# Decay mask of the state-space groups moved into a transfer, and exponentials moved from VectorE to ScalarE

## The chip, the cores and the metric

The kernel runs on one core of a Trainium2 chip. The metric is the time of one execution on the device in microseconds (us). The core's engines work through queues of their own: TensorE (PE, with its weight loads as PEld), VectorE (DVE), ScalarE (ACT), GpSimd (POOL) and SyncE (SP). Transfers are issued by SP, POOL and ACT and carried by 16 DMA engines.

## What is computed

One decoder layer over 512 tokens and 16 learned meta tokens ahead of them, 1024 wide: a normalised input is projected, goes through a pooling branch and a state-space branch (Mamba-2, "SSD"), and the gated sum of both is followed by a feed-forward block. The change lies in the state-space branch. It has 32 heads in 8 groups of 4, works in chunks of 128 tokens, and for each chunk computes

```
a_cs   = cumsum(a_dt)                                  # per head, within the chunk
lmat   = exp(where(l >= s, a_cs[l] - a_cs[s], -inf))   # decay from token s to token l
cb     = c_mat[l] . b_mat[s]                           # per group
y_diag = sum over s of cb * lmat * xdt[s]
y_off  = exp(a_cs[l]) * (c_mat[l] . state)             # state carried from chunk to chunk
y      = (y_diag + y_off + xs * d_skip) * silu(z)
y      = y * rsqrt(mean(y^2 over the group) + 1e-5)    # per group
```

## The kernel before, in words

The projections dominate. Their weights come in blocks of 128x1024 (`raw`, loaded by SP). ACT rounds each block to the upper part `whi` (L111), DVE subtracts to get the lower part `wlo` (L113), and PE multiplies both with the two parts of the input (L215, L218). The results go through a convolution (`conv`: ACT L437, three DVE steps L440, ACT Silu L442).

The eight groups run as `ssd(g)` (L591 to L724), woven with the projections of the next group, `group_proj(g+1)`: while ACT, DVE and POOL prepare group g, PE multiplies for group g+1. Sums of weights (POOL transfers L774 to L783 into `f_t` and `f_s`, among them accumulating ones, L781 and L783) and small copies `seen` that pace them (L797) share POOL's queue. The order of each engine's queue is fixed when the program is built; every engine then works through its own queue strictly in order, so an instruction that waits holds up all behind it.

In `ssd(g)` the path to the diagonal product is this:

- **abc** (128 x 4 x 512, f32; one buffer, so that group g's load has to wait for the last product `py` of group g-1) gets a_cs of the group's four heads, broadcast to all 128 partitions by one POOL transfer (L599). Free axis: token l. Partition: token s of the chunk.
- `eb` = exp(abc), two ACT instructions of 64 partitions each (L633), used by y_off.
- The differences a_cs[l] - a_cs[s], clamped at zero so that no exponential overflows: 8 pieces of 128x128 on ACT (Relu with negative scale, L638), 8 on DVE (L641). Then two exponentials of 128x1024 on ACT (L644, L645). `decay` holds these; in the last group (g7) it is placed behind the copy of the first state (`st`, L667).
- `cbm` = c.b (PE L656) times the triangular mask `tri` (DVE L658): this is where tokens l < s are cut off. Then abc is multiplied with cbm (DVE L676, 128x2048; in g7 in two halves).
- PE multiplies abc with `xdt` into `py` (L691), and the states with `ct` into `po` (L685).

The group's norm: squares and their sums (PE), a Sqrt on ACT (L712) and four reciprocals on DVE (L714) give the factor `rs`; then `yh`/`yl` (L721) are ready for the output product (`pso`, `psp`: L146 to L149).

ACT's functions lie in tables; a change of table shows in the trace as an instruction of its own, ACT_TABLE_LOAD, under the line of the function that needs it.

Of the kernel before, what the change touches and what calls it, by code (L numbers as in the profile page):

```python
# [11 lines left out]
AF = mybir.ActivationFunctionType  # L12
ALU = mybir.AluOpType

P = 128
# [6 lines left out]
G = 8  # L22
R = 4
# [26 lines left out]
X_PAIRS = (4, 5, 6, 7)  # L50
# [14 lines left out]
def kernel(ctx: ExitStack, tc, xT, x, w, fx, f1, f2, vec, fnw, out):  # L65
    nc = tc.nc
    act, dve, pe, pool = nc.scalar, nc.vector, nc.tensor, nc.gpsimd
# [33 lines left out]
    def after(*ins):  # L101
        st = ExitStack()
        for i in ins:
            if i is not None:
                st.enter_context(tc.issue_after(i.ins))
        return st
# [36 lines left out]
    def mm3s(ps, pairs, first=True, last=True):  # L143
# [4 lines left out]
        for n, ((ah, al), (bh, bl)) in enumerate(pairs):  # L148
# [9 lines left out]
    tri = const.tile([P, P], F32, name="tri")  # L158
    pool.affine_select(out=tri, in_=ones_f, compare_op=ALU.is_ge, fill=0.0, base=0,
                       pattern=[[1, P]], channel_multiplier=-1)  # L160
    eps = const.tile([P, 1], F32, name="eps")
    dve.memset(eps, EPS)
    vs = const.tile([P, V_N], F32, name="vs")
# [5 lines left out]
    dtok = const.tile([P, 2, 4, HEADS], F32, name="dtok")  # L169
# [26 lines left out]
    def psum1(name):  # L196
        return psb.tile([P, 512], F32, tag="s", name=name)
# [139 lines left out]
    pn = psum1("pn1")  # L337
    for c in range(6):
        pe.matmul(pn[:NT, c : c + 1], q[:, c * NT : (c + 1) * NT], ones_f[:, :1], start=True, stop=True)
    rs = pre.tile([NT, 6], F32, name="rs")  # L340
# [12 lines left out]
    for i in range(2):  # L353
        pb = psum1(f"pb1_{i}")
        c = slice(3 * i, 3 * i + 3)
# [14 lines left out]
    for c in range(4):  # L370
        r = slice(c * H, (c + 1) * H)
# [22 lines left out]
    acs_d = dram.tile([H, SEQ], F32, name="acs_d")  # L394
    for c in range(4):
        nc.gpsimd.dma_start(acs_d[:, c * P : (c + 1) * P], acs[c * H : (c + 1) * H, :P])
    def dt_out():

        sel = pre.tile([P, 2, P], F32, tag="wdt", name="sel")
        dve.tensor_copy(sel[:, 0, :], ident[:, P - 1 : P].to_broadcast([P, P]))  # L400
        dve.tensor_copy(sel[:, 1, :], ident[:, NM - 1 : NM].to_broadcast([P, P]))
        pt = psum1("pt_dt")
        for j, src in enumerate((dt, acs)):
            pe.transpose(pt[:, j * P : (j + 1) * P], src[:, :P], ident)
            pe.transpose(pt[:NM, 256 + j * H : 256 + (j + 1) * H], src[:H, P:], ident[:H, :H])
        dve.tensor_copy(dtok.rearrange("p a c h -> p (a c h)"), pt[:, :256])
        dve.tensor_copy(dtm.rearrange("p a h -> p (a h)"), pt[:NM, 256 : 256 + 2 * H])
        pq = psum1("pq_dt")
        pe.matmul(pq[:, :128], sel[:, 0, :], dtok[:, 1, :, :].rearrange("p c h -> p (c h)"),
                  start=True, stop=True)  # L410
        pe.matmul(pq[:NM, 128 : 128 + H], sel[:NM, 1, :NM], dtm[:, 1, :], start=True, stop=True)
        fl = lambda t: t.rearrange("p c h -> p (c h)")
        dve.tensor_tensor(fl(dec), pq[:, :128], fl(dtok[:, 1, :, :]), op=ALU.subtract)
        dve.tensor_tensor(wmeta[:NM], pq[:NM, 128 : 128 + H], dtm[:, 1, :], op=ALU.subtract)
        act.activation(fl(dec), fl(dec), AF.Exp)
        act.activation(wmeta[:NM], wmeta[:NM], AF.Exp)
        dve.tensor_tensor(wmeta[:NM], wmeta[:NM], dtm[:, 0, :], op=ALU.mult)
        act.activation(fl(cdec), pq[:, :128], AF.Exp)


    u_d = [dram.tile([P, L], F32, name=f"u_d{k}") for k in range(NK)]
# [10 lines left out]
    x_ready, z_ready, filled = {}, {}, {}  # L432
# [158 lines left out]
    def ssd(g, cur):  # L591

        xc, bt, ct, zt = cur
        hs = slice(R * g, R * g + R)
        tok = lambda c: slice(NM + c * P, NM + (c + 1) * P)
        ctok = lambda c: slice(c * P, (c + 1) * P)
        flat = lambda t: t.rearrange("p r d -> p (r d)")
        abc = gs.tile([P, R, SEQ], F32, tag="abc", name=f"abc{g}")
        abc_load[g] = nc.gpsimd.dma_start(abc, acs_d[hs, :].partition_broadcast(P))  # L599

        xdt = gs.tile([P, 4, R, 64], F32, tag="xdt", name=f"xdt{g}")
        btok = gs.tile([P, 4, P], F32, tag="btok", name=f"btok{g}")
# [23 lines left out]
        if g == G - 1:  # L626
            yield
        eb = gs.tile([P, 2, SEQ], F32, tag="eb", name=f"eb{g}")
        ap = abc.rearrange("p (i j) l -> p i j l", j=2)
        for j in range(2):  # L630
            js = slice(64 * j, 64 * j + 64)
            with after((z_ready if g in X_PAIRS else x_ready)[g], late_cast[0] if g == G - 1 else None):
                act.activation(eb[js, :, :], ap[js, :, j, :], AF.Exp)  # L633
        dm = abc.rearrange("p r (c l) -> p r c l", c=4)
        for r in range(R):
            for c in range(4):
                if r < 2:
                    act.activation(dm[:, r, c, :], dm[:, r, c, :], AF.Relu, scale=-1.0,  # L638
                                   bias=dtok[:, 1, c, R * g + r : R * g + r + 1])
                else:  # L640
                    dve.tensor_scalar(dm[:, r, c, :], dm[:, r, c, :], dtok[:, 1, c, R * g + r : R * g + r + 1],  # L641
                                      0.0, op0=ALU.subtract, op1=ALU.min)
        def decay():
            act.activation(abc[:, :2], abc[:, :2], AF.Exp, scale=-1.0)  # L644
            return act.activation(abc[:, 2:], abc[:, 2:], AF.Exp)  # L645


        if g < G - 1:
            done[g] = decay()
        mark[0] = xdt[:, 0, 0, :1]  # L650
        yield

        pc = psum1(f"pcb{g}")
        with tc.issue_after(filled[g].ins) if g in filled else nullcontext():
            for c in range(4):
                pe.matmul(pc[:, c * P : (c + 1) * P], bt[:, tok(c)], ct[:, ctok(c)], start=True, stop=True)  # L656
        cbm = gs.tile([P, 4, P], F32, tag="cbm", name=f"cbm{g}")
        dve.tensor_tensor(cbm, pc.rearrange("p (c l) -> p c l", c=4),  # L658
                          tri.unsqueeze(1).to_broadcast([P, 4, P]), op=ALU.mult)
        st = [gs.tile([P, R, 64], F32, tag=f"st{c}", name=f"st{c}_{g}") for c in range(4)]  # L660
        pss = [psum1(f"pst{g}_{b}") for b in range(2)]
        pv = [pss[c // 2][:, (c % 2) * 256 : (c % 2) * 256 + 256] for c in range(4)]
# [5 lines left out]
        if g == G - 1:  # L668
            with tc.issue_after(st0.ins):
                decay()  # L670
# [3 lines left out]
        for rs_ in ((slice(0, 2), slice(2, R)) if g == G - 1 else (slice(0, R),)):  # L674
            n = rs_.stop - rs_.start
            masked[g] = dve.tensor_tensor(dm[:, rs_], dm[:, rs_], cbm.unsqueeze(1).to_broadcast([P, n, 4, P]),  # L676
                                          op=ALU.mult)
# [4 lines left out]
        for i in range(2):  # L682
# [5 lines left out]
            for c in range(4):  # L688
                for j in range(2):
                    r = 2 * i + j  # L690
# [6 lines left out]
                                     op0=ALU.mult, op1=ALU.add)  # L697
# [10 lines left out]
        pn = psum1(f"png{g}")  # L708
        pe.matmul(pn, ones_r, qh, start=True, stop=False)
        pe.matmul(pn, ones_r, ql, start=False, stop=True)  # L710
        rs = gs.tile([P, SEQ], F32, tag="cbm", name=f"rs{g}")
        act.activation(rs, pn, AF.Sqrt, bias=eps, scale=1.0 / 256)  # L712
        for c in range(4):
            dve.reciprocal(rs[:, ctok(c)], rs[:, ctok(c)])  # L714
        yield
        for i in range(2):
            y = yt[:, i, :]
# [8 lines left out]
    late_cast, last_state = [None], {}  # L726
    done, abc_load, masked, y_first, squared, b_meta, x_decayed = {}, {}, {}, {}, {}, {}, {}
# [79 lines left out]
    for d in range(GATES_FIRST):  # L807
        gate_pool(d, True)
        if d == 0:
            dt_out()  # L810
# [117 lines left out]
    for g in range(G):  # L928
        nxt = group_tiles(g + 1) if g + 1 < G else None
        fill = [group_proj(g + 1, nxt, GATE_AT.get(g))] if nxt else [out_part()]  # L930
        if g == 4:
            fill = [out_half()] + fill
        weave(ssd(g, cur), fill, 2 if g == 4 else 1, weight_sums_at(SETS_AT[g], PIECES.get(g, 12)),
              [sums_of_u(g)] if g in SUMS_AT else [])
        cur = nxt
# [692 lines left out]
    c = NC - 1  # L1628
# [14 lines left out]
    for t in range(4):  # L1643
        T, st = t // 2, slice((t % 2) * P, (t % 2 + 1) * P)
        n = 0
        for half in range(2):
            parts = [(0, 512)] if half == 0 or t < 3 else [(0, 256), (256, 256)]
            for a, m in parts:
# [3 lines left out]
                i = 0  # L1652
# [179 lines left out]
```

## Time and profile before

| | |
|---|---|
| time before, median of 3 runs | 1004.51 us (1001.51, 1004.57, 1004.51) |
| profiled execution | 1003.26 us, of which the span from first to last instruction is 1001.6 |
| granted TensorE clock | 0.999 |
| PE busy | 989.0 us, 99% of the span |
| DVE busy | 804.2 us, 80% |
| ACT busy | 602.9 us, 60% |
| POOL busy | 121.9 us, 12% |
| DMA | 184.52 MB, mean 184 GB/s |

Times inside the program are us from the start of the span. Groups of instructions are given as "count x | busy time, mean ns of one | idle time of the engine ahead of them <- who ended it". The groups g0 to g7 run from 62 us (transfer of abc in g0) to 455 us (last `py` of g7).

### The profile page before, as it was taken

Reading aid. Unit: us, or ns where it says so; the run is one execution under the profiler, and the core shown is the slowest. Engines: PE = TensorE matmul, PEld = TensorE weight load, DVE = VectorE, ACT = ScalarE, POOL = GpSimd, SP = SyncE. Lnnn points to the kernel's source line nnn. Section 1 sums busy time; section 2 is a strip of 40 time slices with the busy share of each in tenths; the row PEclk is TensorE's granted clock in tenths of the full one; section 3 lists DMA queues with packets and bytes.
Section 4 is the critical chain, followed back from the end, with each engine's and each line's share of the span. In section 5 each row is a group of like instructions: output and inputs, shape, how many; then the busy total and the mean of one; then the engine's idle time right before and its main releaser. Section 6 shows DMA issues by size and latency. Waiting matters only on the chain.

```text
span 1001.6 us, 15673 instructions
## 1 busy us (share of the span) xinstructions
PE 989.0 (99%) x6035; PEld 873.4 (87%) x6035; DVE 804.2 (80%) x1162; ACT 602.9 (60%) x855; POOL 121.9 (12%) x215
## 2 busy tenths in 40 slices
PE   9999999999999999999999999999999999999997
PEld 7889898989889999978898888888889999999986
DVE  7977997879855888978789667876988878888885
ACT  7657749494924658574345443377666666656654
POOL 0010321211212312223200001121000000000000
PEclk9999999999999999999999999999999999999999
DMA  7374868676798849678823732889354464454332
GB/s 245 89 254 140 265 182 238 195 192 199 221 262 265 232 122 278 211 161 172 286 68 127 252 101 77 259 232 323 88 197 149 142 194 138 157 185 151 129 106 84
DMA packets 61803, 184.52 MB, mean 184 GB/s; under 512 B 7072, under 2 KB 8416, under 8 KB 60704
## 3 DMA queue, kind: packets, MB, share of 16 engines
q1 hardware_dynamic: 39456, 109.00, 33.3%
q0 software_dynamic: 18240, 67.51, 26.4%
q10 hardware_dynamic: 4032, 7.00, 1.9%
q8 instruction: 47, 0.77, 0.3%
q14 instruction: 28, 0.23, 0.1%
HBM read 173.13 MB, written 58.59 MB: 231 GB/s over the span
## 4 chain that ended last, share of the span: by engine, by line
PE 84%; DVE 7%; ACT 4%; DMA 3%; issue 1%; SPq 0%; ACTq 0%; DVEq 0%
PE px L1451 8%; PE px L215 7%; PE alpha L1519 6%; PE pz L215 6%; PE px L1454 4%; PE px L218 4%; PE pgp L215 3%; PE alpha L1522 3%; PE pz L218 3%; PE pgs L215 3%; DMA raw<-in_w 2%; PE pqx L506 2%; PE py L691 2%; PE pgp L218 2%; PE pso L146 1%; PE wo_alpha L1213 1%
## 5 line engine op out<-in xcount | busy, mean ns | idle before, releaser
L113 DVE TENSOR_TENSOR wlo<-raw,whi 128x1024 fp32r<-128x1024 f32 (+2 forms) x88 | 102.2, 1171 | 45.0 <-ACT whi L111 29.7
L111 ACT CAST whi<-raw 128x1024 fp32r<-128x1024 f32 (+2 forms) x88 | 87.2, 1012 | 64.0 <-DMA raw<-in_w 15.8
L215 PE MATMUL px<-uh,whi 128*128 128x264 f32 (+1 forms) x320 | 81.1, 291 | 0.0
L218 PE MATMUL px<-ul,whi 128*128 128x264 f32 (+1 forms) x320 | 78.7, 284 | 0.0
L1226 DVE TENSOR_TENSOR ht<-ht,alpha 128x1024 f32<-128x1024 f32 x35 | 42.7, 1220 | 29.1 <-PE alpha L1519 29.1
L215 PEld LDWEIGHTS px<-uh,whi 128*128 128x128 f32 x320 | 60.5, 189 | 1.1 <-issue 0.9
L1149 ACT CAST shi<-rawf 128x1024 fp32r<-128x1024 f32 x42 | 44.2, 1053 | 28.0 <-PE alpha L1522 18.4
L218 PEld LDWEIGHTS px<-ul,whi 128*128 128x128 f32 x320 | 60.2, 188 | 0.4 <-issue 0.2
L1519 PE MATMUL alpha<-shi,hh 128*128 128x512 f32 x140 | 55.3, 395 | 0.7 <-DVE ht L1226 0.6
L1522 PE MATMUL alpha<-shi,hl 128*128 128x512 f32 x140 | 54.7, 391 | 0.0
L1150 DVE TENSOR_TENSOR slo<-rawf,shi 128x1024 fp32r<-128x1024 f32 x42 | 51.2, 1219 | 0.6 <-ACT shi L1149 0.6
L1454 PE MATMUL px<-vsl,shi 128*128 128x256 f32 x192 | 47.4, 280 | 0.0
L1451 PE MATMUL px<-vsh,shi 128*128 128x256 f32 x192 | 47.4, 281 | 0.0
L215 PE MATMUL pz<-uh,whi 128*128 128x512 f32 x112 | 43.8, 391 | 1.7 <-DVE xc L440 1.7
L218 PE MATMUL pz<-ul,whi 128*128 128x512 f32 x112 | 43.6, 390 | 0.0
L215 PE MATMUL px<-uh,wlo 128*128 128x264 f32 (+1 forms) x320 | 42.0, 283 | 0.0
L215 PEld LDWEIGHTS px<-uh,wlo 128*128 128x128 f32 x320 | 40.0, 188 | 0.0
L1519 PE MATMUL alpha<-slo,hh 128*128 128x512 f32 x140 | 37.4, 389 | 0.0
L1451 PEld LDWEIGHTS px<-vsh,shi 128*128 128x128 f32 x192 | 36.2, 188 | 0.9
L1454 PEld LDWEIGHTS px<-vsl,shi 128*128 128x128 f32 x192 | 36.1, 188 | 0.9
L1454 PE MATMUL px<-vl,shi 128*128 128x256 f32 x144 | 36.1, 283 | 0.0
L1451 PE MATMUL px<-vh,shi 128*128 128x256 f32 x144 | 36.0, 282 | 0.0
(599 smaller groups left out, 3068.3 us busy)
## 6 DMA issues: line engine op xcount, KB each, us to landing
raw<-in_w SPq DMA_DIRECT2D x96, 512.0 KB, 4.6
f_t<-in_f POOLq DMA_DIRECT2D x38, 512.0 KB, 7.5
f_s<-in_f POOLq DMA_DIRECT2D x26, 512.0 KB, 7.0
b<-in_f SPq DMA_DIRECT2D x21, 512.0 KB, 4.4
rawf<-in_f SPq DMA_DIRECT2D x36, 256.0 KB, 3.0
rawf<-f_t SPq DMA_DIRECT2D x36, 256.0 KB, 3.1
abc<-acs_d POOLq DMA_DIRECT2D x8, 1024.0 KB, 8.3
f_t<-f_t POOLq DMA_DIRECT2D x12, 512.0 KB, 6.7
```

The source lines that it names most:

```text
L111: act.copy(hi[:, c], raw[:, c])
L113: dve.tensor_tensor(lo[:, c], raw[:, c], hi[:, c].bitcast(F32), op=ALU.subtract)
L215: pe.matmul(o, wt, rhs[0][k][:, c], start=part == 0 and k == 0, stop=part == 1 and k == NK - 1)
L218: mm[0] = pe.matmul(o, wt, rhs[1][k][:, c], start=False, stop=False)
L506: at = pe.matmul(o, wk, f[k][0], start=start and not low and k == 0, stop=stop and low == 1 and k == 3, skip_group_check=True)
L1149: splits.append((act.copy(hi, src), dve.tensor_tensor(lo, src, hi.bitcast(F32), op=ALU.subtract)))
L1150: dve.tensor_tensor(lo, src, hi.bitcast(F32), op=ALU.subtract)))
L1226: added[0] = dve.tensor_tensor(o, o, src, op=op)
L1451: pe.matmul(ps, m, f[k][0], start=start and not low and k == 0, stop=stop and low == 1 and k == 3, skip_group_check=True)
L1454: pe.matmul(ps, m, f[k][1], start=False, stop=False, skip_group_check=True)
L1519: pe.matmul(ps[t], hh[:, p, seg, st], m, start=bool(first and not low and p == 0), stop=bool(last and low and p == 1), skip_group_check=True)
L1522: pe.matmul(ps[t], hl[:, p, seg, st], m, start=False, stop=False, skip_group_check=True)
```

## The change

1. `tri` becomes an additive mask once, at the start: (tri - 1) * 1e30, so 0 where l >= s and -1e30 elsewhere.
2. `dtok[:, 1]` (a_cs with tokens on partitions) is negated once, in `dt_out`, to serve as a bias.
3. Per group, abc is first filled with `tri` (POOL transfer from SBUF, 16 times 128 columns on each partition), then a_cs is added to it by a second, accumulating POOL transfer.
4. `eb` gets two POOL transfers of its own (64 partitions x 2 x 512 each) and one exponential of 128x1024 in place.
5. The 16 differences and the two large exponentials become 16 exponentials of 128x128 with a bias, all on ACT. Both these and eb's are placed behind `z_ready[g]`, the Silu that ends the z part of the projection of group g.
6. `cbm` is a plain copy on ACT.
7. `rs` = exp(-ln(mean + eps)/2), two ACT instructions of 128x512, no reciprocals.

```diff
+    dve.tensor_scalar(tri, tri, 1.0, 1e30, op0=ALU.subtract, op1=ALU.mult)
...
+        dve.tensor_scalar(fl(dtok[:, 1, :, :]), fl(dtok[:, 1, :, :]), -1.0, None, op0=ALU.mult)
...
-        abc_load[g] = nc.gpsimd.dma_start(abc, acs_d[hs, :].partition_broadcast(P))
+        nc.gpsimd.dma_start(abc.rearrange("p r (c l) -> p (r c) l", l=P),
+                            tri.unsqueeze(1).to_broadcast([P, 4 * R, P]))
+        abc_load[g] = nc.gpsimd.dma_start(abc, acs_d[hs, :].partition_broadcast(P), accum_op=ALU.add)
...
-        ap = abc.rearrange("p (i j) l -> p i j l", j=2)
         for j in range(2):
-            js = slice(64 * j, 64 * j + 64)
-            with after((z_ready if g in X_PAIRS else x_ready)[g], late_cast[0] if g == G - 1 else None):
-                act.activation(eb[js, :, :], ap[js, :, j, :], AF.Exp)
+            nc.gpsimd.dma_start(eb[64 * j : 64 * j + 64, :, :],
+                                acs_d[hs, :].rearrange("(i j) l -> j i l", j=2)[j].partition_broadcast(64))
         dm = abc.rearrange("p r (c l) -> p r c l", c=4)
-        for r in range(R):
-            for c in range(4):
-                if r < 2:
-                    act.activation(dm[:, r, c, :], dm[:, r, c, :], AF.Relu, scale=-1.0,
-                                   bias=dtok[:, 1, c, R * g + r : R * g + r + 1])
-                else:
-                    dve.tensor_scalar(dm[:, r, c, :], dm[:, r, c, :], dtok[:, 1, c, R * g + r : R * g + r + 1],
-                                      0.0, op0=ALU.subtract, op1=ALU.min)
         def decay():
-            act.activation(abc[:, :2], abc[:, :2], AF.Exp, scale=-1.0)
-            return act.activation(abc[:, 2:], abc[:, 2:], AF.Exp)
+            for r in range(R):
+                for c in range(4):
+                    with after(z_ready[g]):
+                        at = act.activation(dm[:, r, c, :], dm[:, r, c, :], AF.Exp,
+                                            bias=dtok[:, 1, c, R * g + r : R * g + r + 1])
+            return at
+        def in_decay():
+            with after(z_ready[g], late_cast[0] if g == G - 1 else None):
+                act.activation(eb, eb, AF.Exp)
         if g < G - 1:
             done[g] = decay()
+        in_decay()
...
-        dve.tensor_tensor(cbm, pc.rearrange("p (c l) -> p c l", c=4),
-                          tri.unsqueeze(1).to_broadcast([P, 4, P]), op=ALU.mult)
+        act.copy(cbm.rearrange("p c l -> p (c l)"), pc)
...
-        act.activation(rs, pn, AF.Sqrt, bias=eps, scale=1.0 / 256)
-        for c in range(4):
-            dve.reciprocal(rs[:, ctok(c)], rs[:, ctok(c)])
+        act.activation(rs, pn, AF.Ln, bias=eps, scale=1.0 / 256)
+        act.activation(rs, rs, AF.Exp, scale=-0.5)
```

The order in which the program is built changes at several places. In the first group, on ACT, stands before (columns: line, operation, output <- inputs, shape, count; `bt` and `ct` are g1's B and C projections, `st_0` the first state):

```order
L111 CAST whi_1165<-raw_1164 128x1024
L633 ACT_TABLE_LOAD
L633 ACTIVATE eb_960<-abc_931 64x1024 x2
L638 ACTIVATE abc_931<-abc_931,dtok 128x128 x8
L645 ACTIVATE abc_931<-abc_931 128x1024
L644 ACTIVATE abc_931<-abc_931 128x1024
L442 ACT_TABLE_LOAD
L442 ACTIVATE bt_928<-bt_928 128x528
L667 COPY st_0_1056<-pst_0_1060 128x256
L437 ACTIVATE ct_929<-px_25_1078,vs 128x512
```

And at the same place after the change (lines are those of the changed kernel):

```order
L111 CAST whi_1167<-raw_1166 128x1024
L661 COPY cbm_1056<-pcb_1051 128x512
L669 COPY st_0_1058<-pst_0_1062 128x256
L111 CAST whi_1253<-raw_1252 128x1024
L648 ACT_TABLE_LOAD
L648 ACTIVATE eb_963<-eb_963 128x1024
L444 ACT_TABLE_LOAD
L444 ACTIVATE bt_930<-bt_930 128x528
L642 ACT_TABLE_LOAD
L642 ACTIVATE abc_933<-abc_933,dtok 128x128 x16
L439 ACTIVATE ct_931<-px_25_1080,vs 128x512
```

The exponentials on abc move behind a copy, a cast, eb's exponential, a Silu and two table loads more; `ct`, whose PSUM the projection needs back, stays behind them.

On POOL, around the last group's load of abc (the one of g7; `seen` are the pacing copies, `f_t` and `f_s` the sums of weights), stands before:

```order
L774 DMA f_t_498<-in_f 128x1024
L797 COPY seen<-bt_4162 128x1
L775 DMA f_s_499<-in_f 128x1024
L797 COPY seen<-ct_4163 128x1
L776 DMA f_t_498<-in_f 128x1024
L599 DMA abc_4633<-acs_d 128x2048
L797 COPY seen<-yt_4366 128x1
L778 DMA f_t_500<-in_f 128x1024
```

After the change, from the second of abc's two transfers on (the first, L601, filling abc from `tri`, stands five rows ahead of it):

```order
L780 DMA f_s_500<-in_f 128x1024
L603 DMA abc_4614<-acs_d 128x2048
L798 COPY seen<-xc_4145 128x1
L782 DMA f_t_501<-f_t_499 128x1024
L798 COPY seen<-qhg_4528 128x1
L783 DMA f_t_502<-in_f 128x1024
L798 COPY seen<-qhg_4528 128x1
L634 DMA eb_4672<-acs_d 64x2x512
L798 COPY seen<-qhg_4528 128x1
L775 DMA f_t_503<-in_f 128x1024
L784 DMA f_t_502<-f_t_501 128x1024
L634 DMA eb_4672<-acs_d 64x2x512
```

One transfer of abc has become two with transfers of weights between them, and the second half of eb stands behind an accumulating transfer (L784, which is L783 before).

Counted over the whole program, ACT has 48 table loads in its order after, 43 before: in each group the Ln and the Exp of `rs` have one each, where the Sqrt had one. PE has the same products, and SP the same transfers in the same order; on PE, the first `py` products of g0 stood among the last products of `px_2` (a projection of g1) and stand behind them now.

## The prediction

> **What bounds the kernel now.** I read the busy times first, then the stage of the eight groups by itself, then what TensorE waits for.
>
> From the page's first part (busy us, share, instructions), and the window from 75 to 475 us (length, then busy us with counts of PE, PEld, DVE, ACT and POOL, granted clock, DMA share, GB/s):
>
> ```profile
> PE 989.0 (99%) x6035; PEld 873.4 (87%) x6035; DVE 804.2 (80%) x1162; ACT 602.9 (60%) x855; POOL 121.9 (12%) x215
> 75.00:475.00 400.00, 396.52 (x2644) 355.99 (x2643) 321.02 (x494) 260.84 (x360) 90.37 (x158) 1.00 0.75 209
> ```
>
> TensorE is busy 396.5 of 400 us in the stage that the change touches, and the change takes no product from it. VectorE has 79 us free there, ScalarE 139. What a change off TensorE can win is at most the 3.5 us that TensorE idles. Its waits (us in total, times, longest) name the large ones of this stage:
>
> ```profile
> PE pz L215 <- DVE xc L440: 1.7, 1, 1.7
> PE psp L146 <- ACT sp L868: 1.4, 1, 1.4
> PE po L685 <- ACT st L667: 0.2, 1, 0.2
> ```
>
> 1.7 + 1.4 + 0.2 = 3.3 us; the other waits of the page lie before or behind the stage. So I ask of each part only this: does some operand of TensorE come later than TensorE reaches it?
>
> **Work on VectorE and ScalarE.** The groups by line (count | busy us, mean ns | idle before):
>
> ```profile
> L714 DVE RECIPROCAL rs<-rs 128x128 f32<-128x128 f32 x32 | 27.2, 911 | 7.9 <-ACT rs L712 7.8
> L641 DVE TENSOR_SCALAR abc<-abc,dtok 128x128 f32<-128x128 f32 x64 | 14.0, 282 | 0.9 <-ACT eb L633 0.8
> L658 DVE TENSOR_TENSOR cbm<-pcb,tri 128x512 f32<-128x512 f32 x8 | 5.5, 689 | 6.4 <-PE pcb L656 6.3
> L638 ACT ACTIVATE abc<-abc,dtok 128x128 f32<-128x128 f32 x64 | 20.2, 392 | 0.2
> L633 ACT ACTIVATE eb<-abc 64x1024 f32<-64x1024 f32 x16 | 17.0, 1060 | 0.3
> L644 ACT ACTIVATE abc<-abc 128x1024 f32<-128x1024 f32 x8 | 8.4, 1052 | 0.0
> L712 ACT ACTIVATE rs<-png,eps 128x512 f32<-128x512 f32 x8 | 5.5, 690 | 0.2
> L712 ACT ACT_TABLE_LOAD x8 | 10.3, 1283 | 0.1
> L608 ACT COPY btok<-ptb 128x512 f32<-128x512 f32 x8 | 4.6, 580 | 0.5 <-PE ptx L619 0.5
> ```
>
> VectorE loses 27.2 + 14.0 + 5.5 = 46.7 us, 5.8 a group. ScalarE loses, a group, 20.2/8 = 2.5 (the eight differences), 2.1 (eb) and 2 x 1.05 (the exponentials; L645 costs what L644 does): 6.7 us. It gains 16 exponentials of 128x128, for which I take the rate of the differences, 2.46 us for 8 in a row (row of g0 below), so 4.9; one exponential of 128x1024 for eb, 1.06; the copy of cbm, 0.58 as btok's; one more pass over rs, 0.69. That is 7.2, +0.5 us a group, or 4 in all, and by the orders 48 - 43 = 5 more table loads, 5 x 1.283 = 6.4. These 10 us lie beside TensorE, in ScalarE's 139 free us, and cost nothing by themselves; without that cover they would cost all 10. The two new VectorE instructions at the start (tri, the sign of dtok) are each no larger than a 128x128 step, 0.28 us, beside work that TensorE does for the start: nothing.
>
> Beside the row of 1283 ns stands a rule: the Trainium skill, "ScalarE: Activation LUTs", section "Table sets: the hidden batching unit", has one set with both ln and exp, so that Ln followed by Exp needs one load. By it each group would save a load (8 x 1.283 us of ScalarE) and the sum below would fall by 0.7 us at g1; the order of the changed program shows two loads, and it decides.
>
> **The transfer of abc.** Its prices before (KB, median us from issue to landing; the second and third row of abc are the windows 188 to 200 and 372 to 386 us, the quickest and the slowest; then POOL's own time to issue):
>
> ```profile
> abc<-acs_d POOLq DMA_DIRECT2D x8, 1024.0 KB, 8.3
> f_t<-f_t POOLq DMA_DIRECT2D x12, 512.0 KB, 6.7
> abc<-acs_d POOLq DMA_DIRECT2D x1, 1024.0 KB, 5.1
> abc<-acs_d POOLq DMA_DIRECT2D x1, 1024.0 KB, 11.4
> L396 POOL DMA_DIRECT2D acs_d<-dacs x4 | 2.2, 561 | 47.5 <-DVE dacs L393 47.5
> L599 POOL DMA_DIRECT2D abc<-acs_d x8 | 4.5, 561 | 25.1 <-PE py L691 14.6 <-DVE xt L425 10.5
> ```
>
> Now tri is spread over abc in 128 x 16 = 2048 pieces of 512 B, and only when that has landed may a_cs be added. No row shows so many pieces. Issuing 32 pieces (L396) and 128 pieces (L599) takes POOL the same 0.56 us. From below, tri costs the quickest megabyte, 5.1 us. From above, if every 32 pieces cost POOL 0.56 us, 64 x 0.56 = 36 us. The rows that are nearest say that the number of pieces does not count, while the load on the DMA engines does (5.1 against 11.4 for the same megabyte): I take 10. The accumulating megabyte lies between 5.1 and two accumulating half megabytes, 13.4; I take 10. So abc is there 20 us after the previous group's last `py`, instead of 8.3. Bounds: 10 and 49.
>
> One sentence of the skill bears on this: "DMA: Bandwidth & Descriptors", section "Anatomy of one DMA — SWDGE (gpsimd) path", gives 2.0 us plus bytes/436e3, an estimate of 4.4 us for a megabyte, and little cost for many descriptors; the row's 5.1 at best and 8.3 at the median stand against it, and by it abc would be there after 9 us and the sum would be some 2 us less.
>
> When is abc wanted? The load is issued when the previous group's `py` ends (issues: min, median, max ns of one, first and last start, within 95 to 430 us; the window from 370 to 440 holds g6's and g7's; then g2's first use of abc, as start, us):
>
> ```profile
> L599 POOL DMA_DIRECT2D abc<-acs_d x7: 535/567/577, 98.7 to 415.8; - x7
> L599 POOL DMA_DIRECT2D abc<-acs_d x2: 567/572/577, 373.4 to 415.8; - x2
> 143.67 0.54 POOL L599 DMA_DIRECT2D abc<-acs_d  x1
> 172.50 1.06 ACT L644 ACTIVATE abc<-abc 128x1024 f32<-128x1024 f32 x1
> ```
>
> g2: issued 143.7, there at 164, exponentials at 172.5: 9 us of slack. In g3 to g5 the times between are longer still. These groups cost nothing at 20 us. The tight ones are g0, g1, g6 and g7.
>
> **g0.** Start, us, engine, line:
>
> ```profile
> 79.12 1.03 ACT L111 CAST whi<-raw 128x1024 fp32r<-128x1024 f32 x1
> 83.64 2.46 ACT L638 ACTIVATE abc<-abc,dtok 128x128 f32<-128x128 f32 x8
> 86.95 1.04 ACT L644 ACTIVATE abc<-abc 128x1024 f32<-128x1024 f32 x1
> 88.02 2.29 DVE L676 TENSOR_TENSOR abc<-abc,cbm 128x2048 f32<-128x2048 f32 x1 [2.83 <-ACT abc L644]
> 90.68 0.87 PE L691 MATMUL py<-abc,xdt 128*64 128x128 f32 x10
> ```
>
> The mask ended at 90.3, 0.4 us ahead of `py`. In the new order, from 80.2 (cast done): cbm 0.6, st 0.35, a cast 1.0 give 82.1; then load, eb, load, bt, load (3 x 1.28 + 1.06 + 0.65 = 5.6) give 87.7; sixteen exponentials give 92.6, the mask 94.9. TensorE, whose `py` now stands behind px_2, comes there at about 93.1: a stall of 1.8 us. `ct` waits behind the exponentials, its PSUM is back at about 98, and TensorE's next block of projections with it. Behind that stood the wait of 1.7 us for xc (pz), which absorbs part: pz starts at about 105.9 instead of 105.1. **+0.9**, between -1 (the pz wait goes, VectorE being freer) and +4 (nothing is absorbed).
>
> **g1 and g6.** First g1, then g6:
>
> ```profile
> 123.81 1.06 ACT L645 ACTIVATE abc<-abc 128x1024 f32<-128x1024 f32 x1
> 127.05 2.29 DVE L676 TENSOR_TENSOR abc<-abc,cbm 128x2048 f32<-128x2048 f32 x1
> 132.90 1.09 PE L691 MATMUL py<-abc,xdt 128*64 128x128 f32 x16
> 400.55 1.05 ACT L645 ACTIVATE abc<-abc 128x1024 f32<-128x1024 f32 x1
> 403.53 2.29 DVE L676 TENSOR_TENSOR abc<-abc,cbm 128x2048 f32<-128x2048 f32 x1
> 405.92 1.09 PE L691 MATMUL py<-abc,xdt 128*64 128x128 f32 x16
> ```
>
> g1: abc is there at 98.7 + 20 = 119; the exponentials come behind Ln, Exp and a load each, at about 123, and end at 128. The order puts bt's convolution ahead of the mask, so that it runs from 131.9 to 134.2; TensorE, moved by g0, comes at 133.8, and the rest of the stall (0.4) and the Silu behind it make **+0.7**. From 123 on, each us that abc comes later costs one. g6: issued 373.4, there at 393.4; eb and the exponentials follow at 394 to 400, the mask ends about 405.0, within 0.9 of `py` at 405.9. In the crowded stretch of 11.4 us per megabyte it is there at 396 to 397 and half of that is late: **+0.9**.
>
> **g7.**
>
> ```profile
> 435.33 0.83 POOL L783 DMA_DIRECT2D f_t<-f_t  x1 [6.04 <-DMA f_t<-in_f]
> 436.77 2.14 ACT L633 ACTIVATE eb<-abc 64x1024 f32<-64x1024 f32 x2
> 445.44 1.05 ACT L868 COPY sp<-psp 128x512 f32<-128x512 f32 x2
> 446.06 0.50 PE L146 MATMUL psp<-yh,whi 128*128 128x512 f32 x1 [1.44 <-ACT sp L868]
> ```
>
> The second half of eb is queued behind L783, which waits for its own source until 435.3; issued at 436.2, landing in the quickest case 5 us later, 441. Before, eb was computed from abc at 436.8. ScalarE waits about 1.5 us at eb, and st, the exponentials and sp wait behind it, and TensorE for st and sp: **+1.3**, between -1.4 (the sp wait goes) and +4.
>
> **Contention.** tri and eb add 1.5 MB a group. The stage's DMA share of 0.75 would rise towards 0.9, and loads of raw weights, for which ScalarE sometimes waits, land later: **+1**, between 0 and +5.
>
> Sum: 0.9 + 0.7 + 0.9 + 1.3 + 1.0 = 4.8 us. Against the profiled execution, 1003.26 us (span 1001.6 and 1.7 around it), this gives 1008.1; that execution lies 1.25 below the median of the runs, 1004.51, so the medians' difference may look smaller by that.
>
> **The rivals.** *Hidden anyway (no change).* abc arrives within 10 to 15 us, the stalls at g0 and g7 take the place of the waits of 1.7 and 1.4 there, and nothing is added: 1002 to 1005.5. For it: 139 free us on ScalarE. Against it: the order of g0, where `ct` and `py` both stand behind the exponentials. *Slow transfer (slower still).* The 2048 pieces cost more than their bytes. From 123 us on at g1, and 397 at g6, ScalarE stands at its first exponential, with everything behind it (casts of weights too), and TensorE with it. With tri at 25 us, abc is there after 35: g1 at 134, 11 late, g6 at 408, 11 late, g2 6 late, g7 at 451, some 8 late beyond its `py` at 446.5: 20 to 30 us with part absorbed, 1012 to 1040. It decides from 15 us for tri. *Faster.* VectorE, 5.8 us a group freer, ends xc's convolution ahead of pz, and ScalarE reaches sp in time: the 3.3 us of waits go and no stall comes, 1003.3 - 3.3 = 1000, and at best 998 with PE's small gaps. Against it: the g0 order. *The change does not do what it says:* Ln and Exp were to replace a load and four reciprocals, but bring a load more; that is in the sum.
>
> **How the numbers follow.** Forecast (1005.5 to 1012) 0.44, hidden 0.27, slow transfer 0.17, faster 0.12. The likeliest gives 1008.1. The range reaches from 1000.5, which leaves out half of the faster case, to 1028, which leaves out the upper third of the slow one. A measurement of this kernel can tell 0.3%, 3 us, from no change: faster is below 1001.5, slower above 1007.5. Of the forecast's 0.44, 0.10 lie below 1007.5: same 0.27 + 0.10 = 0.37, slower 0.34 + 0.17 = 0.51, faster 0.12.
>
> **What would show it.** In the profile after: abc's landing, 20 us after `py`, against 10 or 35; a wait of `py` for abc (VectorE) at 93 us of some 1.8; g2 to g5 without waits; a ScalarE wait for a DMA at eb in g7; a DMA share near 0.9; VectorE near 760 us busy, ScalarE near 613. The forecast falls if tri's transfer takes POOL or the DMA engines longer than 15 us, or if TensorE's waits in the stage stay near 3.3.

## The result, and the profile after

The changed kernel takes 1045.74 us (median of 4 runs, 1044.17 to 1047.83) against 1003.18 us of the kernel before (the three runs of the table above and a fourth, 1001.86): a ratio of 1.0428, 95% interval [1.0413, 1.0444]. The forecast was 1008.1. The profiled span is 1043.2 us, 41.6 us longer than before.

The busy times and the stage from 75 to 475 us, to be read beside the same two rows of before:

```profile
PE 999.5 (96%) x6035; PEld 881.6 (85%) x6035; DVE 762.7 (73%) x1060; ACT 612.0 (59%) x916; POOL 138.0 (13%) x239
```

```profile
75.00:475.00 400.00, 373.81 (x2479) 336.82 (x2477) 256.65 (x358) 245.98 (x380) 94.57 (x168) 0.97 0.82 226
```

VectorE and ScalarE have the work that was reckoned (762.7 and 612.0 us). TensorE has the same 6035 products, but idles 1043.2 - 999.5 = 43.7 us where it idled 12.6, and is busy 10.5 us longer with them: 31.1 + 10.5 = 41.6, the whole loss. The granted clock in the stage is 0.97 in place of 1.00. (The groups now end later: g7's stall reaches to 484 us, beyond this window.)

What TensorE waits for now, and what ScalarE waits for (us in total, times, longest):

```profile
PE po L687 <- ACT st L669: 16.7, 3, 12.0
PE po L687 <- DVE st L675: 9.5, 4, 3.3
PE py L693 <- issue: 4.9, 3, 1.8
PE pz L216 <- DVE xc L442: 1.5, 1, 1.5
```

```profile
ACT eb L648 <- DMA eb<-acs_d: 18.4, 3, 10.9
ACT whi L111 <- DMA raw<-in_w: 16.3, 9, 4.4
```

The big wait is for `st`, a copy of 0.37 us. ScalarE makes it late because it stands at eb's exponential, ahead of it in the queue, for a transfer of 256 KB. The transfers (KB, median us to landing) from the page's group of DMA issues:

```profile
abc<-tri POOLq DMA_DIRECT2D x8, 1024.0 KB, 6.9
abc<-acs_d POOLq DMA_DIRECT2D x8, 1024.0 KB, 11.2
```

```profile
eb<-acs_d POOLq DMA_DIRECT2D x16, 256.0 KB, 12.4
```

At the median, the fill in 2048 pieces lands sooner than the accumulating megabyte, and the small transfers of eb, a quarter of the fill's size, take nearly twice as long as the fill. The last group shows the whole chain in three timelines (start, us, engine, line; in brackets the idle time ahead and who ended it): POOL, ScalarE, TensorE.

```profile
457.66 0.90 POOL L603 DMA_DIRECT2D abc<-acs_d  x1 [5.55 <-DMA abc<-tri]
...
470.88 0.86 POOL L784 DMA_DIRECT2D f_t<-f_t  x1 [8.42 <-DMA f_t<-in_f]
471.44 0.94 POOL L634 DMA_DIRECT2D eb<-acs_d  x1
```

```profile
480.51 1.06 ACT L648 ACTIVATE eb<-eb 128x1024 f32<-128x1024 f32 x1 [10.94 <-DMA eb<-acs_d]
481.47 1.03 ACT L847 CAST whi<-raw 128x1024 fp32r<-128x1024 f32 x1
482.40 0.58 ACT L661 COPY cbm<-pcb 128x512 f32<-128x512 f32 x1
482.88 1.04 ACT L847 CAST whi<-raw 128x1024 fp32r<-128x1024 f32 x1
483.83 0.37 ACT L669 COPY st<-pst 128x256 f32<-128x256 f32 x1
```

```profile
484.25 0.80 PE L687 MATMUL po<-ct,st 128*128 128x128 f32 x2 [12.02 <-ACT st L669]
```

POOL waits 5.55 us for the fill and 8.42 for a transfer of weights before it can issue the second half of eb, which then takes 9 us to land; ScalarE waits 10.94, TensorE 12.02. In g6 ScalarE waits 2.4 us for abc and then 3.2 for eb, whose second half POOL could issue only after 8.0 us of waiting for a transfer of weights. In g1 it is the landing, in a stretch in which POOL's queue is full: from 104 to 133 us, these transfers were issued, among others.

```profile
raw<-in_w SPq DMA_DIRECT2D x4, 512.0 KB, 11.6
abc<-acs_d POOLq DMA_DIRECT2D x1, 1024.0 KB, 13.7
fx_t<-fx_t POOLq DMA_DIRECT2D x2, 512.0 KB, 9.4
fx_t<-in_fx POOLq DMA_DIRECT2D x2, 512.0 KB, 10.7
fx_s<-in_fx POOLq DMA_DIRECT2D x1, 512.0 KB, 15.0
eb<-acs_d POOLq DMA_DIRECT2D x2, 256.0 KB, 15.8
```

### The profile page after: what moved, and what is told of

It is laid out like the page before. It is cut to its first block, busy times and chain, and to the rows that moved or that the text cites. A ratio compares the mean times of both kernels' runs of the same rounds, so it can differ in the third digit from the quotient of the medians.

```text
span 1043.2 us, 15699 instructions
## 1 busy us (share of the span) xinstructions
PE 999.5 (96%) x6035; PEld 881.6 (85%) x6035; DVE 762.7 (73%) x1060; ACT 612.0 (59%) x916; POOL 138.0 (13%) x239
## 3 DMA queue, kind: packets, MB, share of 16 engines
q1 hardware_dynamic: 39456, 109.00, 31.1%
## 4 chain that ended last, share of the span: by engine, by line
PE 72%; DMA 11%; DVE 6%; ACT 6%; issue 4%; POOL 1%; SPq 0%; ACTq 0%; DVEq 0%; POOLq 0%
PE px L1452 8%; PE alpha L1520 6%; PE px L1455 4%; PE px L216 4%; PE alpha L1523 3%; DMA eb<-acs_d 3%; DMA f_t<-in_f 3%; PE pgs L216 2%; PE pgp L216 2%; PE pz L216 2%; PE px L219 2%; PE py L693 2%; PE pso L146 1%; DMA rawp<-fx_t 1%; PE wo_alpha L1214 1%
## 5 line engine op out<-in xcount | busy, mean ns | idle before, releaser
L687 PE MATMUL po<-ct,st 128*128 128x128 f32 x128 | 23.1, 303 | 26.3 <-ACT st L669 16.7
L687 PEld LDWEIGHTS po<-ct,st 128*128 128x128 f32 x128 | 19.2, 207 | 29.4 <-ACT st L669 17.6
L442 DVE SCALAR_TENSOR_TENSOR bt<-px,vs,bt 128x527 f32<-128x527 f32 (+2 forms) x21 | 16.0, 761 | 36.2 <-ACT bt L439 36.1
L642 ACT ACTIVATE abc<-abc,dtok 128x128 f32<-128x128 f32 x128 | 38.7, 389 | 2.4 <-DMA abc<-acs_d 2.4
## 6 DMA issues: line engine op xcount, KB each, us to landing
abc<-acs_d POOLq DMA_DIRECT2D x8, 1024.0 KB, 11.2
```

Source lines behind the costliest of these rows:

```text
L687: pe.matmul(po[:, c * P : (c + 1) * P], flat(st[c])[:, i * P : (i + 1) * P], ct[:, ctok(c)], start=True, stop=True)
```

## The experiments

Theory A is that the change is slow because of its transfers, B that it is slow because of ScalarE's and TensorE's new order. Times are medians; each ratio is against runs of the kernel before on the same chip (1002.7 to 1003.7 us).

**Without eb's transfers.**

```diff
-        for j in range(2):
-            nc.gpsimd.dma_start(eb[64 * j : 64 * j + 64, :, :], ...)
+                act.activation(eb[js, :, :], ap[js, :, j, :], AF.Exp)   # from abc, ahead of the sixteen
```

> The changed kernel without eb's two own transfers: eb is again the exponential of rows of abc, in two instructions of 64 partitions, ahead of the sixteen; the tri transfer and the accumulating transfer stay (eb then holds masked values, which leaves the right eb out). Theory A (the change is slow because of its transfers: ScalarE stands at eb for 18.4 us in g1, g6 and g7, and the weights come late in g2 and g3 because of the second megabyte): the 18.4 us and the low clock behind them go, the rest stays, 1018 to 1026 us. Theory B (the new order on ScalarE is what costs: differences only behind z_ready, and cbm and st behind sixteen exponentials and eb): 1040 to 1048, since eb's exponentials get longer, not shorter.

1029.23 us, ratio 1.0261 [1.0242, 1.0279]: 17 us of the 43 are gone, a little less than A expected (3 us above its range).

**With the plain load of abc, and with both edits.**

```diff
-        nc.gpsimd.dma_start(abc..., tri.unsqueeze(1).to_broadcast([P, 4 * R, P]))
-        abc_load[g] = nc.gpsimd.dma_start(abc, acs_d[hs, :].partition_broadcast(P), accum_op=ALU.add)
+        abc_load[g] = nc.gpsimd.dma_start(abc, acs_d[hs, :].partition_broadcast(P))
...
-                                            bias=dtok[:, 1, c, R * g + r : R * g + r + 1])
+                                            bias=eps)
```

> The changed kernel with abc loaded by one plain transfer as before, no fill from tri and no accumulating; the sixteen exponentials take the column eps as bias (this leaves out the mask and the differences, all instructions keep their size); eb keeps its two own transfers. Theory A: the software queue has 1 MB a group less ahead of eb and the weights are in time in g2 and g3; g7's wait for eb stays since that one stands behind an accumulating transfer of weights: 1008 to 1025. Theory B: 1038 to 1046.

> Both edits together: one plain transfer of abc, eb from abc, bias eps (no mask, no differences). What is left of the change is the work on ScalarE and VectorE and its order. Theory A: nothing of the loss is left, 1002 to 1008. Theory B: 1030 to 1046.

Plain load: 1012.28 us, 1.0084 [1.0063, 1.0105]. Both: 1015.19 us, 1.0121 [1.0101, 1.0140]. Theory A takes most of the loss; but 8 to 12 us stay that no added transfer of abc explains, so B holds for a part. With the plain load eb's own transfers do little harm (ScalarE waits 2.9 us for them in all, in place of 18.4):

```profile
abc<-acs_d POOLq DMA_DIRECT2D x8, 1024.0 KB, 7.0
eb<-acs_d POOLq DMA_DIRECT2D x16, 256.0 KB, 6.1
```

They land in 6.1 us in place of 12.4. So in this order of the engines eb's cost is what the other transfers make of it.

**The norm alone.** The kernel before with one edit:

```diff
-        act.activation(rs, pn, AF.Sqrt, bias=eps, scale=1.0 / 256)
-        for c in range(4):
-            dve.reciprocal(rs[:, ctok(c)], rs[:, ctok(c)])
+        act.activation(rs, pn, AF.Ln, bias=eps, scale=1.0 / 256)
+        act.activation(rs, rs, AF.Exp, scale=-0.5)
```

> The kernel before with the norm factor alone changed: Ln and Exp on ScalarE in place of Sqrt and the four reciprocals. Theory A: 1000 to 1006, VectorE 27 us less busy, beside TensorE. Theory B: slower by 3 to 8 us, since one more table load and pass stand on ScalarE ahead of yh.

1003.96 us, 1.0012 [1.0000, 1.0025], with VectorE busy 778.2 us. 26 us of VectorE's work bought nothing, and the table loads cost next to nothing.

**Which of abc's two transfers.** First the fill by VectorE, then the second transfer without accumulating (with eps as bias of the exponentials, so without mask and differences).

```diff
-        nc.gpsimd.dma_start(abc.rearrange("p r (c l) -> p (r c) l", l=P), ...)
+        dve.tensor_copy(abc.rearrange("p r (c l) -> p (r c) l", l=P), ...)
```

```diff
-        abc_load[g] = nc.gpsimd.dma_start(abc, acs_d[hs, :].partition_broadcast(P), accum_op=ALU.add)
+        abc_load[g] = nc.gpsimd.dma_start(abc, acs_d[hs, :].partition_broadcast(P))
```

> The changed kernel with abc filled from tri by one VectorE copy of 128x2048 a group in place of the transfer; the accumulating transfer and eb's own transfers stay. Nothing is left out. Theory C (the fill transfer is what costs: it comes first in line and holds the accumulating one, POOL's queue behind that, and the DMA engines): near the plain load's 1012, say 1010 to 1018. Theory D (the accumulating transfer is what costs, being dearer than a plain one and reading its target): 1028 to 1042.

> The changed kernel with both transfers of abc, but the second one overwrites in place of accumulating, and the exponentials take eps as bias (this leaves out the mask and the differences). Theory C: as slow as the change within 6 us, 1038 to 1048. Theory D: 1010 to 1025, since the second megabyte is then as cheap as the plain load.

1031.80 us, 1.0278 [1.0259, 1.0297], and 1030.12 us, 1.0275 [1.0246, 1.0305]. The first lies in D's range, the second between those of C and D. Each takes about 15 us away, so neither the fill nor the accumulating is the one culprit. Both profiled executions are above their medians (1040.88 and 1035.41 us), so their traces give no sizes of stalls. In the second one eb's landing falls with the second megabyte's:

```profile
abc<-acs_d POOLq DMA_DIRECT2D x8, 1024.0 KB, 8.9
eb<-acs_d POOLq DMA_DIRECT2D x16, 256.0 KB, 9.9
```

**eb's exponential behind the state's copy.**

```diff
             done[g] = decay()
-        in_decay()
...
         y_first[g] = st0 = act.copy(flat(st[0]), pv[0])
+        with tc.issue_after(st0.ins):
+            in_decay()
```

> The changed kernel with eb's exponential placed behind the copy of the first state on ScalarE; all transfers stay. If eb's late landing costs only because cbm and st are queued behind eb's exponential on ScalarE, the waits of TensorE for st go in g1, g6 and g7 and the time comes to that of the run with eb from abc, 1024 to 1032. If the late landing costs by itself (yt waits for eb, and the PSUM of po and py with it), 1038 to 1048.

1026.75 us, 1.0232 [1.0201, 1.0262]. All transfers are there, eb lands as late as before the edit (13.2 us), and 19 us are gone: it was the place in ScalarE's queue. What TensorE still waits for:

```profile
PE py L694 <- issue: 10.4, 2, 9.1
PE po L688 <- DVE st L676: 7.6, 6, 2.8
```

The wait for ScalarE's st is gone; the 9.1 us are `py` in g7, whose exponentials stand behind eb's.

**eb through another queue.**

```diff
-            nc.gpsimd.dma_start(eb[64 * j : 64 * j + 64, :, :], ...)
+            nc.scalar.dma_start(eb[64 * j : 64 * j + 64, :, :], ...)
```

> The changed kernel with eb's two transfers issued by ScalarE, so that they go through another queue than the fill, the accumulating transfer and the sums of weights. Nothing is left out. If eb is late because it stands behind those in the software queue (12.4 us for 256 KB), it now lands in 3 to 5 us and ScalarE's 18 us of waiting for eb go: 1024 to 1032. If it is late because the DMA engines are busy, it stays near 10 us and the time at 1038 to 1046.

1022.26 us, 1.0180 [1.0158, 1.0202]. The time is 2 us better than expected, but not for the expected reason: landing takes 8.1 us, not 3 to 5. The gain is in the issue. Rows of the second half in g6 and of both halves in g7, from ScalarE's timeline:

```profile
393.16 0.58 ACTq L634 DMA_DIRECT2D eb<-acs_d  x1
...
443.17 1.29 ACTq L634 DMA_DIRECT2D eb<-acs_d  x2
```

Here the second half goes out 11 us after the group's fill (which POOL issued at 381.8 in g6 and 432.5 in g7); in the changed kernel 25 us after it (395.2 to 420.6 and 446.0 to 471.4), because POOL's queue stood waiting for the fill and for weights. ScalarE's waits for eb fall from 18.4 us to 4.8 (2.4 at the exponential, 2.4 at the table load ahead of it).

**Both cures of eb.** The last two edits together.

> The changed kernel with both cures of eb: its transfers issued by ScalarE, its exponential behind the copy of the first state. Nothing is left out. If both cures work on the same 18 us of waiting, 1018 to 1024, no better than the queue alone (1022). If the stalls of TensorE at st that were left (5 us) go too, 1012 to 1017.

1014.85 us, 1.0118 [1.0098, 1.0138], with fill, accumulating transfer and eb's transfers all in place and nothing left out. The cures add up further: 31 of the 43 us were eb, the lower clock behind its stalls included. What is left is as long as in the run without both transfers (1.0121), but not for the same reason. ScalarE now waits for abc, 3.2 us in g0 and 3.4 in g6, and TensorE idles 2.8 and 3.8 us behind that (`py` in g0, `po` in g6):

```profile
ACT abc L642 <- DMA abc<-acs_d: 6.6, 2, 3.4
PE po L688 <- DVE st L676: 5.4, 3, 3.8
PE py L694 <- issue: 2.8, 1, 2.8
```

The run without both transfers has no wait of ScalarE for abc. So the fill and the accumulating transfer still cost something here, and that the totals agree doesn't show that they are free.

**Load on the DMA engines alone.** The kernel before with a transfer a group of the fill's size, from tri to memory, that nothing waits for; in the first run free to go at any time, in the second behind abc's load.

```diff
+        scratch = dram.tile([P, 4 * R, P], F32, name=f"scratch{g}")
+        with tc.issue_after(abc_load[g].ins):      # second run only
+            nc.gpsimd.dma_start(scratch, tri.unsqueeze(1).to_broadcast([P, 4 * R, P]))
```

> The kernel before, with one more transfer a group of the fill's size and pieces, from tri to a scratch buffer in memory, issued behind abc's load; nothing waits for it. Only the load on the DMA engines and POOL's queue is left. If that is what costs: 1010 to 1020. If it is the chain of fill, load and use: 1001 to 1006.

> The kernel before with the extra transfer of the fill's size from tri to a scratch buffer in memory, now held in its group: it is issued behind abc's load of the same group (in the run before, all eight were issued at the start of the program). Nothing waits for it. If load on the DMA engines and on POOL's queue by itself makes the weights late: 1008 to 1018. If extra transfers cost only through what waits for them: 1001 to 1005.

1026.51 us, 1.0235 [1.0220, 1.0251], and 1004.40 us, 1.0009 [0.9998, 1.0020]. The first run doesn't answer its question: with nothing to hold them, all eight transfers went out at the start of the program,

```profile
L601 POOL DMA_DIRECT2D scratch<-tri x8: 1111/1121/1361, 1.9 to 27.6; - x8
```

where they were in the way of the loads that TensorE needs first. The second one does: the same megabytes in their groups cost nothing that can be measured (2 us at most, by the interval).

```profile
abc<-acs_d POOLq DMA_DIRECT2D x8, 1024.0 KB, 8.2
scratch<-tri POOLq DMA_DIRECT2D x8, 1024.0 KB, 12.4
```

(They go to memory and stand behind abc's load; the fill writes to SBUF and stands ahead of it.) A megabyte more a group is not by itself the cost; waiting for it is.

**Fill and eb in the kernel before.** The fill, then the plain load over it; and eb by its own transfers, all else as before.

```diff
+        nc.gpsimd.dma_start(abc.rearrange("p r (c l) -> p (r c) l", l=P),
+                            tri.unsqueeze(1).to_broadcast([P, 4 * R, P]))
         abc_load[g] = nc.gpsimd.dma_start(abc, acs_d[hs, :].partition_broadcast(P))
```

```diff
         for j in range(2):
-            js = slice(64 * j, 64 * j + 64)
-            with after((z_ready if g in X_PAIRS else x_ready)[g], ...):
-                act.activation(eb[js, :, :], ap[js, :, j, :], AF.Exp)
+            nc.gpsimd.dma_start(eb[64 * j : 64 * j + 64, :, :], ...)
+        with after((z_ready if g in X_PAIRS else x_ready)[g], ...):
+            act.activation(eb, eb, AF.Exp)
```

> The kernel before, with abc first filled from tri by the transfer of the change and then overwritten by the plain load, which has to wait for the fill. Nothing else changes. If groups g2 to g5 have the slack that the profile of before showed (9 us and more from landing to use), the fill costs only in g1, g6 and g7: 1003 to 1010. If the fill delays the weights and what else stands behind it in POOL's queue, every group pays: 1015 to 1025 (the fill made 18 us of difference in the changed kernel).

> The kernel before, with eb loaded by its two own transfers and one exponential of 128x1024. If eb's transfers cost only behind the longer queue of the change: 1002 to 1008, most of it at g7 where the second half stands behind an accumulating transfer. If they cost by themselves, 1012 to 1022.

1012.97 us, 1.0105 [1.0073, 1.0137], and 1037.54 us, 1.0345 [1.0328, 1.0361]. The first lies between the two ranges. Its largest new stalls are 2.1 us at `py` in g0 and 3.8 us in g1, where VectorE stood 5.7 us at the differences on abc, ahead of an operand that TensorE needed. The second is outside both ranges, a surprise. eb's transfers land in 6.6 us, but ScalarE waits for them as long as in the changed kernel: 15.5 us at the table load and 2.9 at the exponential. And in the kernel before, eb's exponential, gated by the projection, stood at the head of abc's work; without it the differences are put earlier in the queues of ScalarE and VectorE, which then stand waiting for abc too:

```profile
ACT L633 <- DMA eb<-acs_d: 15.5, 3, 5.7
ACT abc L638 <- DMA abc<-acs_d: 12.8, 6, 3.7
```

In the kernel before ScalarE has no wait for abc among its rows; in the changed kernel, with the gate on z_ready, it has one of 2.4 us. How much of the 35 us is eb's and how much the differences', this run doesn't tell. It does show that a landing of some 6 us isn't harmless everywhere: it depends on what stands behind the wait.

**What stays: gates or chain.** Both edits (no added transfer) with the gates of before; cbm's copy on VectorE with the plain load; and the mask added by VectorE after a plain load, nothing left out.

```diff
-                    with after(z_ready[g]):
+                    with nullcontext():
...
-                with after(z_ready[g], ...):
+                with after((z_ready if g in X_PAIRS else x_ready)[g], ...):
                     act.activation(eb[js, :, :], ap[js, :, j, :], AF.Exp)
```

> The run without both transfers (plain load, eb from abc, no mask, no differences; 1015.2 us), with the gates of before: eb behind the Silu of x or z as in the kernel before, the sixteen exponentials without a gate. If the remaining 12 us come from everything standing behind z_ready, 1003 to 1008. If they come from ScalarE's longer chain (sixteen exponentials and cbm ahead of st), 1011 to 1018.

```diff
-        act.copy(cbm.rearrange("p c l -> p (c l)"), pc)
+        dve.tensor_copy(cbm.rearrange("p c l -> p (c l)"), pc)
```

> The kernel with the plain load of abc (no mask, no differences, eps as bias; 1012.3 us) with the copy of cbm on VectorE in place of ScalarE. If ScalarE's length between z and st is what the remaining 8 us are (cbm's 0.58 us stands ahead of st in each group), the loss falls by a third or more, 1006 to 1010. If they come from the differences standing behind z_ready, nothing changes: 1011 to 1014.

```diff
         in_decay()
+        dve.tensor_tensor(abc..., abc..., tri.unsqueeze(1).to_broadcast([P, 4 * R, P]), op=ALU.add)
```

> The mask without any transfer: abc loaded by the plain transfer, eb from abc, tri then added by VectorE (one 128x2048 step a group, 2.3 us), sixteen exponentials with bias, cbm copied by ScalarE. Nothing is left out. If only the transfers and the gates cost, it comes to the run without both transfers, 1013 to 1018. VectorE's add stands between eb and the exponentials, which adds 2.3 us to the chain: if the chain decides, 1018 to 1026.

Gates of before: 1011.49 us, 1.0082 [1.0066, 1.0099], 4 us less than 1.0121. cbm on VectorE: 1011.69 us, 1.0081 [1.0056, 1.0106], no change from 1.0084. VectorE's add: 1013.46 us, 1.0100 [1.0085, 1.0115]. So a third of the 12 us is the gates. The rest, 7.8 us by the profiled spans, is 4.5 us more idle time of TensorE and 3.3 us more busy time; the run with the gates of before shows these largest stalls in the stage:

```profile
PE pz L216 <- DVE xc L442: 2.7, 1, 2.7
PE po L685 <- DVE st L673: 1.6, 4, 0.9
PE po L685 <- ACT st L667: 1.2, 1, 1.2
```

The first stood at 1.7 in the kernel before. They weren't taken apart further. No version here is faster than the kernel before.

## Why the prediction was wrong, point by point

- **The bound.** Right: at most 3.5 us could be won, and 41.5 us less of VectorE (804.2 to 762.7) won none. The run with the norm alone shows it for the largest part.
- **Work on ScalarE and VectorE.** Right: 612.0 and 762.7 us busy against 613 and near 760.
- **The transfers of abc.** The sum was right, its two terms only roughly: 10 + 10 forecast, 6.9 + 11.2 at the median, 7 to 13 and 9 to 14 at the three tight groups. abc was there 21 us after `py` in g1, 23 in g6 and 21 in g7, where 20 had been reckoned. By the Trainium skill ("DMA: Bandwidth & Descriptors", "Anatomy of one DMA — SWDGE (gpsimd) path") the estimate was 4.4 us for a megabyte; both medians are above it. Its word that many descriptors cost little agrees with the 1.2 us that POOL took to issue the fill. The rival of the slow transfer was wrong in its reason (tri at 15 us or more), though its times come nearest. One row was misread: 172.5 was not g2's first use of abc in the kernel before, eb read it at 161.8 and the differences at 167.8. The slack holds all the same, as the changed kernel takes abc first in its sixteen exponentials, at 182.5 in g2 and without a wait.
- **g0.** The stall at `py` was 1.2 us, 1.8 forecast, and the pz wait stayed at 1.5.
- **g1, g6 and g7: the step that failed.** eb's transfers were priced at g7 alone, at 1.3 us: "issued at 436.2, landing in the quickest case 5 us later". Two errors are in that. POOL's times were taken over from the profile of before, although the change puts a wait for the fill into that very queue: POOL issued the second half at 471.4, 25 us after the fill of the group, where the kernel before issued L783 19.5 us after abc's load and needed no eb. And the quickest landing was taken where 256 KB take 12.4 us behind two megabytes and the sums. In g1 and g6 eb was not priced at all; ScalarE stood 4.3 and 3.2 us there. The order had shown that eb stands ahead of cbm and st on ScalarE; what it meant for TensorE was worked out for abc, and not for eb. TensorE's stalls there came to 5.2, 6.1 and 12.0 us where 0.7, 0.9 and 1.3 had been forecast; in g6 abc's own lateness (ScalarE stood 2.4 us for it) has a part. The run with both cures of eb puts a price on the step: 31 us.
- **g2 to g5, nothing.** Half wrong: abc had the slack, but TensorE waited 3.3 us each in g2 and g3 for st, which VectorE could make only after ScalarE's copy. ScalarE stood there for weights that landed late, 4.4 us in g2 and 5.2 in g3, with the exponentials queued behind. These are ScalarE's timelines at the two places:

```profile
172.84 1.05 ACT L111 CAST whi<-raw 128x1024 fp32r<-128x1024 f32 x1 [4.38 <-DMA raw<-in_w]
```

```profile
226.12 1.05 ACT L111 CAST whip<-rawp 128x1024 fp32r<-128x1024 f32 x1 [5.16 <-DMA rawp<-in_fx]
```

- **Contention, +1.** The second scratch run says that a megabyte more a group costs nothing by itself; in the changed kernel, where fill, accumulating transfer and eb meet, the weights were late twice. With eb's transfers issued by ScalarE and all else in place, ScalarE has no wait for weights in g2 and g3, and TensorE no stall above 0.4 us. In the run without eb's transfers, waits of 2.1 and 3.3 us for weights stay there. So eb in POOL's queue is needed for the full delay, but it isn't the only cause.
- **What was not in the sum at all:** the stalls of g1, g3, g6 and g7 are followed by stretches at a lower clock (last section), 10.5 us in all.
- **The small stalls** of the forecast, 4.8 us, have no run of their own. The runs without the transfers lose 8 to 12 us, but partly at other places (pz 1 us longer, `st` in g7) and without eb's and contention's part of the sum, so they don't confirm it.

## What to carry to other kernels

In this kernel a new transfer was priced by its place in its queue more than by its size: read what its issuing engine will be waiting for after the change, not before it, and then what stands behind the first instruction that needs it. A small operand whose consumer isn't urgent belongs behind the urgent copies on an in-order engine; moving one exponential behind one copy gave back 19 us. Relief of an engine off the bound bought nothing here, and a stall put on the bound could cost more than its length.

## What the runs showed of the hardware

**A stall can be paid twice.** After most of the longer stalls of TensorE the granted clock was low, while TensorE was busy again. Windows around g1's stall in the changed kernel (span, length, busy us and counts of PE, PEld, DVE, ACT and POOL, granted clock, DMA share, GB/s):

```profile
126.00:132.00 6.00, 6.00 (x49) 5.87 (x48) 0.00 (x0) 1.73 (x6) 1.21 (x3) 1.00 0.80 270
132.00:141.00 9.00, 3.84 (x26) 3.00 (x26) 7.03 (x10) 5.86 (x8) 0.51 (x2) 0.82 0.53 120
141.00:146.00 5.00, 5.00 (x30) 4.67 (x28) 3.80 (x9) 1.32 (x3) 0.84 (x3) 0.64 0.67 205
146.00:160.00 14.00, 14.00 (x114) 13.23 (x113) 11.08 (x18) 5.74 (x8) 5.62 (x10) 1.00 0.72 186
```

TensorE idles 5.2 us of the second window, and is then granted 0.64 of its clock for the third, in which it is busy throughout. After the stall of g2 (3.3 us, in the first of these windows) the clock stayed at 1.00; after the one of g3, just as long, it was 0.52:

```profile
190.00:194.50 4.50, 1.17 (x10) 0.85 (x10) 4.50 (x6) 1.42 (x2) 0.00 (x0) 1.00 0.03 9
194.50:199.00 4.50, 4.50 (x46) 4.33 (x47) 4.36 (x10) 1.74 (x3) 0.70 (x2) 1.00 0.52 160
244.00:249.00 5.00, 1.68 (x12) 1.27 (x12) 5.00 (x7) 2.43 (x4) 0.00 (x0) 0.80 0.00 0
249.00:254.00 5.00, 5.00 (x31) 4.67 (x28) 4.43 (x10) 0.98 (x2) 0.83 (x2) 0.52 0.79 273
```

Over the whole program, in windows of 4 us, TensorE's busy time times the part of the clock that was missing adds up to 10.8 us, and to nothing in the kernel before: this is the 10.5 us by which the same products were busy longer.

The Trainium skill ("TensorE: Matmul & The Clock Gate", "Part 1: The HAM clock gate") has the clock at half after an idle window of some 3.4 us. The half agrees: in the third window above products of 264 columns started 0.22 us apart where they start 0.12 apart otherwise. The length doesn't decide alone: 3.3 us had no effect in g2 and halved the clock in g3, the 2.8 us ahead of `py` in g0 of the run with both cures of eb were followed by 5 us at 0.50, and g1's idle time came in three pieces of 1.6 to 1.8 us with a few products between them. What decides between equal stalls, these runs don't show.

**Pieces are cheap to issue.** The fill, 2048 pieces of 512 B by the program, took POOL 1.2 us to issue, where the plain load in 128 pieces took 0.56 (before) and the accumulating one 0.88:

```profile
L601 POOL DMA_DIRECT2D abc<-tri x8: 1182/1201/1221, 61.5 to 446.0; - x8
L603 POOL DMA_DIRECT2D abc<-acs_d x8: 868/884/967, 73.9 to 457.7; - x8
```

That says little about small packets: by the counts of DMA packets in the kernel before and in the run without eb's transfers (61803 and 63979), the eight fills added 272 packets each, some 4 KB a packet.
